# Block sums of the normed input made by 128-feature quarters in five shared buffers, with the homes of three pools turned round

## The chip, the cores and the metric

The kernel runs on one NeuronCore of a Trainium2 chip. Its engines are TensorE (PE in the profile, with its weight loads as PEld), VectorE (DVE), ScalarE (ACT), GpSimd (POOL) and SyncE (SP), which here only issues transfers. Each engine works through its own instructions in the order in which they were written for it, and an instruction that waits for another engine or for a transfer holds everything behind it on its engine. The metric is the device time of one execution in microseconds (us).

## The reference

One layer of a hybrid decoder on 1024 tokens of width 1024 in float32: sandwich norms around two token mixers (a sparse attention and a latent attention) that are merged by sigmoid gates, and around a gated convolutional feed-forward. What matters here is the input projection and the gates:

```python
h = _rmsnorm(x, g_pre_mix[i])
proj = h @ w_in[i]
q_n, kv_n, gate_n, c_q, c_kv, k_r, merge = jnp.split(proj, offsets, axis=-1)
...
gm = jax.nn.sigmoid(merge.astype(jnp.float32)).astype(x.dtype).reshape(B, T, 2, D)
merged = gm[:, :, 0] * (o_nsa @ w_br_nsa[i]) + gm[:, :, 1] * (o_mla @ w_br_mla[i])
```

`merge` has 2048 columns: sixteen output blocks of 128.

## The kernel before

The normed input h is held transposed, features on partitions: `hh` is its high part and `hl` what is left (a float32 value is multiplied as three products of high and low parts, `mm3`, lines 303 to 305). Both stand in two halves of 512 tokens, `hh0`/`hl0` and `hh1`/`hl1`, each of 8 blocks of 128 features.

The stage in question comes after the first token projections. In order of the program:

- the first gate block (`fproj(merge_evac(0))`);
- the latent attention's projections (lines 597 to 652): for each of 8 blocks of 128 tokens `mla_q` and `mla_qt` make queries (tile `qx`), `mla_v` values (`vm`) and `mla_k` keys (`kx`). Each of the three tiles has two buffers, is split into high and low part by ACT and DVE, and is then stored to DRAM by SP (`q_d`, `v_d`, `k_d`);
- three more gate blocks by plain projections, the early projections (`EARLY`, 48 matmuls of 512 columns each);
- ten gate blocks in five pairs by class `Seven`. A pair is a 2 by 2 product of blocks (two gate blocks, two halves of the features, two halves of the tokens) done with seven block products P1 to P7 of 12 matmuls each where eight would be plain (Strassen's scheme in Winograd's form). The products take sums of weight blocks (`S0` to `S3`, line 170, split into `rh`/`rl`, held in a ring of four) and sums of blocks of h: `T1` = B12 - B11, `T2` = B22 - T1, `T3` = B22 - B12, `T4` = B21 - T2, each again as high and low part of 128 x 4 x 512. P5 takes T1, P6 takes T2, P7 takes T3, P4 takes T4; P1, P2 and P3 take plain blocks of h. The T blocks are made once (`t_block`, lines 671 to 678) and serve all five pairs.

A T block is made by DVE and ACT: three DVE operations for the sum (lines 675, 676 and 677: high parts, then each low part), then the split (`split_evac`: ACT copies the high part, line 308, and DVE subtracts it, line 309). Before the change each of these works on 1024 elements per partition, two of the four feature blocks.

The written program is put in order, engine by engine, when it is built: a scheduler places instructions by priority and by what it reckons to be ready. So an edit at one place also changes the order at others.

Memory is handed out by pools that grow from two sides. The pools of the latent attention (`a0`, `a2`) grow from the right and are closed when it is written out. Those of the gates (`tA` for the T blocks, `ringA` for the ring and one weight buffer, `eA` for sums and partial results) grow from the left, into the room that the others leave. A tile that comes to lie where an older tile lay waits until the older one has been read for the last time: by TensorE for weights and inputs, by the store for `qx`, `kx` and `vm`.

Of the kernel before, what the change touches and what calls it, by code (L numbers as in the profile page):

```python
# [8 lines left out]
F32 = mybir.dt.float32  # L9
F32R = mybir.dt.float32r  # L10
# [27 lines left out]
def f32(a):  # L38
    return a.bitcast(F32)
# [236 lines left out]
def tile_hybrid_layer(ctx: ExitStack, tc: tile.TileContext, x, p, positions, g_pre_mix, w_in,  # L276
# [30 lines left out]
    def split_evac(hi, lo, ps):  # L307
        nc.scalar.activation(hi, ps, AF.Copy)  # L308
        nc.vector.tensor_sub(lo, ps, f32(hi))  # L309
# [94 lines left out]
    def two_banks():  # L404
        return ps1([128, 2, 512], F32, "sc", bufs=2)

    hp = Pool("hp", side="right")
    hh, hl = [None, None], [None, None]
# [152 lines left out]
    def fproj(evac):  # L561
        fproj2([evac])

    def merge_evac(m):
        hold = {}

        def run(c, cs, ps):
            if c == 0:
                hold["t"] = gmp([128, T], F32, "gms", bufs=2)
            nc.scalar.activation(hold["t"][:, cs], ps, AF.Sigmoid)  # L570
            if c == 1:
                nc.scalar.dma_start(gm_d[m], hold["t"])
        return run
# [84 lines left out]
    a0.close()  # L658


    tA = Pool("tA", side="left")
    ringA = Pool("ringA", side="left")
    eA = Pool("eA", side="left")
    BA = {n: [tA([128, 4, 512], F32R, n + tag) for tag in "hl"] for n in ("T1", "T2", "T3", "T4")}
    for c in range(2):
        for h in range(2):
            ks = slice(4 * h, 4 * h + 4)
            BA[f"B{h + 1}{c + 1}"] = hh[c][:, ks], hl[c][:, ks]
    gates7 = Seven(nc, W, gate_pairs, ringA, BA, mm3, split_evac)

    def t_block(out_, plus, minus):
        for ks in (slice(0, 2), slice(2, 4)):
            (ah, al), (bh, bl) = ([f32(b[:, ks]) for b in BA[n]] for n in (plus, minus))
            sum_ = eA([128, 2, 512], F32, "sum")
            nc.vector.tensor_tensor(sum_, ah, bh, op=OP.subtract)
            nc.vector.tensor_tensor(sum_, sum_, al, op=OP.add)
            nc.vector.tensor_tensor(sum_, sum_, bl, op=OP.subtract)
            split_evac(BA[out_][0][:, ks], BA[out_][1][:, ks], sum_)

    fproj(merge_evac(EARLY[0]))  # L680
    t_block("T1", "B12", "B11")
    fproj(merge_evac(EARLY[1]))
    t_block("T2", "B22", "T1")
    t_block("T3", "B22", "B12")
    fproj(merge_evac(EARLY[2]))
    for i in range(4):
        gates7.block_sum(0, i)
    for n in range(Seven.RING):
        gates7.prep(n)
    t_block("T4", "B21", "T2")  # L690
    for f in range(len(gate_pairs)):
        tl = [gmp([128, T], F32, "gms", bufs=2) for _ in range(2)]
        gates7.pair(f, two_banks(), bank, eA, [(c[:, :512], c[:, 512:]) for c in tl],
                    lambda out_, ps: nc.scalar.activation(out_, ps, AF.Sigmoid), lambda s: None)
        nc.scalar.activation(tl[1], tl[1], AF.Sigmoid)
        nc.scalar.dma_start(gm_d[PAIRED[2 * f + 1]], tl[1])
        nc.scalar.activation(tl[0][:, 512:], tl[0][:, 512:], AF.Sigmoid)
        nc.scalar.dma_start(gm_d[PAIRED[2 * f]], tl[0])
    for pl in (eA, ringA, tA):
        pl.close()  # L700


# [579 lines left out]
    T1 = []  # L1282
# [32 lines left out]
    for t in (4, 5, 6, 7, 0, 1, 2, 3):  # L1315
        c, lt = t // 4, slice(t % 4 * 128, t % 4 * 128 + 128)
# [212 lines left out]
    left, right = slice(0, 512), slice(512, 1024)  # L1529
# [207 lines left out]
```

## Time and profile before

| | |
|---|---|
| time, median of 3 runs | 1796.21 us (1796.06 to 1799.11) |
| the profiled execution: time, span of its trace | 1803.28 us, 1801.3 us |
| PE busy, share of the span | 1720.6 us, 96% |
| DVE busy | 1274.0 us, 71% |
| ACT busy | 860.7 us, 48% |
| POOL busy | 310.7 us, 17% |

The profiled execution is one run with the profiler on; the median comes from runs of their own. All positions below are microseconds from the start of the trace. TensorE is the engine that is busy nearly throughout, so the question for any stage is where it stands still or runs at the lower of its two clock levels (1.2 and 2.4 GHz).

### The profile page before, as it was taken

What the parts mean: (1) busy time and instruction counts of PE and PEld (TensorE: products, weight loads), DVE (VectorE), ACT (ScalarE), POOL (GpSimd) and SP (SyncE); (2) the same over time, 40 slices, a digit from 0 to 9 for tenths busy, and PEclk for the clock granted to TensorE, in tenths of its full rate; (3) what the DMA queues carried; (4) which work ended last, traced back from release to release, by engine and by line L of the source; (5) the groups of instructions that cost most, each with busy time, mean ns of one, the idle gap of its engine ahead of it and who ended that gap; (6) DMA issues with size and microseconds to landing.
All of it is one profiled execution on the core that took longest, in us unless ns stands there. A gap on an engine that the chain in (4) does not pass through costs nothing.

```text
span 1801.3 us, 23532 instructions
## 1 busy us (share of the span) xinstructions
PE 1720.6 (96%) x8525; PEld 1403.2 (78%) x8525; DVE 1274.0 (71%) x1978; ACT 860.7 (48%) x1532; POOL 310.7 (17%) x467
## 2 busy tenths in 40 slices
PE   8998899999999999999989989999999998999998
PEld 6876678887777787887778867888888876887886
DVE  6456654435888887777764797888888879768453
ACT  6443232235777776666542444444444443345321
POOL 3220003003545544333311000000000000001010
PEclk9999799999999999999999989999999999999999
DMA  5393233200001316757372112222223292438111
GB/s 192 93 281 110 70 110 84 54 28 26 1 1 36 100 59 170 164 136 197 118 245 85 47 59 83 82 82 84 80 82 94 71 345 87 149 118 273 57 59 47
DMA packets 182511, 191.93 MB, mean 107 GB/s; under 512 B 12804, under 2 KB 136124, under 8 KB 182396
## 3 DMA queue, kind: packets, MB, share of 16 engines
q1 hardware_dynamic: 175292, 180.91, 32.9%
q10 hardware_dynamic: 7104, 9.54, 1.6%
q8 instruction: 67, 1.10, 0.3%
q14 instruction: 48, 0.39, 0.1%
HBM read 142.96 MB, written 47.45 MB: 106 GB/s over the span
## 4 chain that ended last, share of the span: by engine, by line
PE 75%; DVE 10%; DMA 8%; ACT 3%; issue 2%; POOL 1%; SPq 1%; DVEq 0%; POOLq 0%; ACTq 0%
PE big L304 9%; PE big L303 9%; PE big L305 9%; PE pT L303 5%; PE pT L304 5%; PE pT L305 5%; PE pT L885 5%; PE one L303 3%; PE one L304 3%; PE one L305 3%; PE oT L895 3%; PE oT L894 3%; PE sc L948 1%; DVE wlo L309 1%; DMA g<-gm_d 1%
## 5 line engine op out<-in xcount | busy, mean ns | idle before, releaser
L345 POOL TENSOR_SCALAR stat<-stat 128x1 f32<-128x1 f32 (+1 forms) x48 | 19.1, 399 | 904.7 <-ACT yn L1278 633.0
L309 DVE TENSOR_TENSOR pl<-pT,ph 128x512 fp32r<-128x512 f32 (+1 forms) x244 | 149.7, 630 | 13.8 <-ACT ph L308 12.0
L308 ACT ACTIVATE ph<-pT 128x512 fp32r<-128x512 f32 (+1 forms) x244 | 130.3, 556 | 60.5 <-PE pT L885 52.7
L303 PE MATMUL big<-hh,rh 128*128 128x512 f32 x364 | 142.3, 391 | 2.2 <-ACT e L220 0.8
L305 PE MATMUL big<-hh,rl 128*128 128x512 f32 x364 | 141.7, 390 | 1.0 <-DVE rl L309 1.0
L304 PE MATMUL big<-hl,rh 128*128 128x512 f32 x364 | 141.9, 390 | 0.0
L869 DVE TENSOR_REDUCE mx<-sc 128x1 f32<-128x640 f32 (+7 forms) x128 | 106.6, 835 | 32.2 <-PE sc L948 22.3
L308 ACT ACTIVATE rh<-S 128x512 fp32r<-128x512 f32 x104 | 65.1, 628 | 120.6 <-PE big L304 80.4
L308 ACT ACTIVATE rh<-wraw 128x512 fp32r<-128x512 f32 x82 | 51.3, 631 | 131.7 <-PE big L304 43.0
L1395 DVE SCALAR_TENSOR_TENSOR u<-C,wcT,u 128x1024 f32<-128x1024 f32 x88 | 110.8, 1279 | 3.6 <-ACT u L1391 3.5
L304 PE MATMUL big<-wlo,whi 128*128 128x512 f32 x242 | 97.3, 402 | 9.4 <-DVE wlo L309 9.3
L305 PE MATMUL big<-whi,wlo 128*128 128x512 f32 x242 | 95.5, 395 | 0.0
L303 PE MATMUL big<-whi 128*128 128x512 f32 x242 | 92.1, 397 | 2.9 <-ACT whi L308 2.9
L303 PE MATMUL pT<-hh,whi 128*128 128x512 f32 x224 | 88.6, 395 | 4.1 <-ACT gms L570 1.6
L305 PE MATMUL pT<-hh,wlo 128*128 128x512 f32 x224 | 87.9, 392 | 0.0
L304 PE MATMUL pT<-hl,whi 128*128 128x512 f32 x224 | 87.8, 392 | 0.0
L309 DVE TENSOR_TENSOR rl<-S,rh 128x512 fp32r<-128x512 f32 x104 | 71.0, 686 | 21.2 <-ACT rh L308 21.2
L303 PEld LDWEIGHTS big<-hh,rh 128*128 128x128 f32 x364 | 68.4, 188 | 17.7 <-ACT e L220 1.2
L305 PEld LDWEIGHTS big<-hh,rl 128*128 128x128 f32 x364 | 68.6, 188 | 15.7 <-DVE rl L309 1.4
L304 PEld LDWEIGHTS big<-hl,rh 128*128 128x128 f32 x364 | 68.5, 188 | 14.5 <-DVE hl L309 0.4
L309 DVE TENSOR_TENSOR rl<-wraw,rh 128x512 fp32r<-128x512 f32 x82 | 56.2, 687 | 21.1 <-ACT rh L308 21.1
L308 ACT ACTIVATE whi<-wraw 128x1024 fp32r<-128x1024 f32 x40 | 42.1, 1058 | 56.9 <-DVE wraw L1464 27.2
(544 smaller groups left out, 5035.4 us busy)
## 6 DMA issues: line engine op xcount, KB each, us to landing
wraw<-in_w_up_dram SPq DMA_DIRECT2D x44, 512.0 KB, 3.9
wraw<-in_w_in_dram SPq DMA_DIRECT2D x24, 512.0 KB, 3.9
g<-gm_d SPq DMA_DIRECT2D x48, 256.0 KB, 3.1
wraw<-in_w_down_dram SPq DMA_DIRECT2D x47, 256.0 KB, 3.3
g_d<-u SPq DMA_DIRECT2D x22, 512.0 KB, 2.6
wraw<-g_d SPq DMA_DIRECT2D x36, 256.0 KB, 3.5
xt<-in_x_dram SPq DMA_DIRECT2D x16, 512.0 KB, 7.5
gm_d<-gms ACTq DMA_DIRECT2D x16, 512.0 KB, 3.4
```

What stands on the lines that cost most here:

```text
L303: nc.tensor.matmul(ps, lh, rh, start=start, stop=False, skip_group_check=more)
L304: nc.tensor.matmul(ps, lh, rl, start=False, stop=False, skip_group_check=more)
L305: nc.tensor.matmul(ps, ll, rh, start=False, stop=stop, skip_group_check=more)
L308: nc.scalar.activation(hi, ps, AF.Copy)
L309: nc.vector.tensor_sub(lo, ps, f32(hi))
L345: nc.gpsimd.tensor_scalar(st, st, EPS, None, op0=OP.add)
L869: nc.vector.tensor_reduce(u.nm[:, r:r + 1], src, axis=AX.XY, op=OP.max, negate=True)
L885: nc.tensor.transpose(pT[:m, r], cols(r), ident)
L894: nc.tensor.matmul(oT[:, a:], v, ph, start=first, stop=False)
L895: nc.tensor.matmul(oT[:, a:], v, pl, start=False, stop=last)
L948: nc.tensor.matmul(ps[:, si, :w], q_part(0, 128, i, 4 * g + r), KA[b - 1][g][:, k0 + o:k0 + o + w], start=False, stop=True)
L1395: nc.vector.scalar_tensor_tensor(u[s], C[s][:, 2 - sh:2 - sh + T], wcT[:, 2 - sh, ch:ch + 1], u[s], op0=OP.mult, op1=OP.add)
```

## The change

The sums are made by quarters: 512 elements per partition instead of 1024, four rounds per T block instead of two. The sum tile, which was one buffer of 128 x 2 x 512, becomes five rotating buffers of 128 x 512 under the name `e`, and the partial results of the pairs (`e1`, `U2`, `U3`), which had buffers of their own, rotate through the same five. `T3` is written after the third early projection and the first weight sums instead of before. The three pools are opened in another order, and the T tiles in the order T2, T3, T4, T1.

```diff
+    eA = Pool("eA", side="left")
+    ringA = Pool("ringA", side="left")
     tA = Pool("tA", side="left")
-    ringA = Pool("ringA", side="left")
-    eA = Pool("eA", side="left")
-    BA = {n: [tA([128, 4, 512], F32R, n + tag) for tag in "hl"] for n in ("T1", "T2", "T3", "T4")}
+    BA = {n: [tA([128, 4, 512], F32R, n + tag) for tag in "hl"] for n in ("T2", "T3", "T4", "T1")}
...
     def t_block(out_, plus, minus):
-        for ks in (slice(0, 2), slice(2, 4)):
-            (ah, al), (bh, bl) = ([f32(b[:, ks]) for b in BA[n]] for n in (plus, minus))
-            sum_ = eA([128, 2, 512], F32, "sum")
+        for k in range(4):
+            (ah, al), (bh, bl) = ([f32(b[:, k]) for b in BA[n]] for n in (plus, minus))
+            sum_ = eA([128, 512], F32, "e", bufs=5)
             nc.vector.tensor_tensor(sum_, ah, bh, op=OP.subtract)
             nc.vector.tensor_tensor(sum_, sum_, al, op=OP.add)
             nc.vector.tensor_tensor(sum_, sum_, bl, op=OP.subtract)
-            split_evac(BA[out_][0][:, ks], BA[out_][1][:, ks], sum_)
+            split_evac(BA[out_][0][:, k], BA[out_][1][:, k], sum_)
...
     t_block("T2", "B22", "T1")
-    t_block("T3", "B22", "B12")
     fproj(merge_evac(EARLY[2]))
     for i in range(4):
         gates7.block_sum(0, i)
     for n in range(Seven.RING):
         gates7.prep(n)
+    t_block("T3", "B22", "B12")
     t_block("T4", "B21", "T2")
     for f in range(len(gate_pairs)):
         tl = [gmp([128, T], F32, "gms", bufs=2) for _ in range(2)]
-        gates7.pair(f, two_banks(), bank, eA, [(c[:, :512], c[:, 512:]) for c in tl],
+        gates7.pair(f, two_banks(), bank, lambda shape, dt, name: eA(shape, dt, "e", bufs=5), [(c[:, :512], c[:, 512:]) for c in tl],
                     lambda out_, ps: nc.scalar.activation(out_, ps, AF.Sigmoid), lambda s: None)
...
-    for pl in (eA, ringA, tA):
+    for pl in (tA, ringA, eA):
         pl.close()
```

The homes, as the built programs place them, in thousands of bytes per partition from the left edge of the room. The older tiles are those of the latent attention. Below 16.9 lie none of them.

| | before | after |
|---|---|---|
| older tiles | | wuh, wul 16.9 to 29.2; wk, wv 29.2 to 37.4; qm, ra, rb 37.4 to 47.6; vm 47.6 to 55.8; kx 55.8 to 64.0; qx 64.0 to 80.4; cth 80.4 to 92.7; ctl 92.7 to 105.0 (same in both) |
| sums and partial results | 94.2 to 104.4 (ctl) | 0 to 10.2 (none) |
| weight buffer of the ring | 65.5 to 69.6 (qx) | 10.2 to 14.3 (none) |
| S0 to S3 | 69.6 to 77.8 (qx) | 14.3 to 22.5 (wuh, wul) |
| rh, rl | 77.8 to 94.2 (qx, cth, ctl) | 22.5 to 38.9 (weights, qm) |
| T1 | 0 to 16.4 (none) | 88.1 to 104.4 (cth, ctl) |
| T2 | 16.4 to 32.8 (wuh, wul, wk) | 38.9 to 55.3 (qm, ra, rb, vm) |
| T3 | 32.8 to 49.2 (wk, wv, qm, ra, rb, vm) | 55.3 to 71.7 (vm, kx, qx) |
| T4 | 49.2 to 65.5 (vm, kx, qx) | 71.7 to 88.1 (qx, cth) |

Three places show how the order moves. The first is on DVE, where the latent attention begins: `krx` is the last split of the token projections, `wul`, `wkl` and `wvl` are splits of the latent attention's weights, `wlo` splits weights of the early projections, `vm_892` is the first tile to be stored. Before:

```order
L309 TENSOR_TENSOR krx_775<-pT_768,krx_775 32x128
L309 TENSOR_TENSOR wul_844<-wraw_247,wuh_843 128x768
L309 TENSOR_TENSOR wul_844<-wraw_251,wuh_843 128x768
L309 TENSOR_TENSOR wkl_846<-wraw_783,wkh_845 128x512
L309 TENSOR_TENSOR wvl_848<-wraw_783,wvh_847 128x512
L107 TENSOR_TENSOR wlo_1315<-wraw_851,whi_1314 128x1024
L309 TENSOR_TENSOR vm_892<-pT_888,vm_892 128x8x64
```

After, from the same split on (behind these rows follow `wvl`, the four L677 of T1, a `wlo`, two `qm` operations and a second `wlo`, and then `vm_892`):

```order
L309 TENSOR_TENSOR krx_775<-pT_768,krx_775 32x128
L675 TENSOR_TENSOR e_1380<-hh1_122,hh0_124 128x512
L675 TENSOR_TENSOR e_1386<-hh1_122,hh0_124 128x512
L675 TENSOR_TENSOR e_1392<-hh1_122,hh0_124 128x512
L675 TENSOR_TENSOR e_1398<-hh1_122,hh0_124 128x512
L676 TENSOR_TENSOR e_1380<-e_1380,hl1_123 128x512
L309 TENSOR_TENSOR wul_844<-wraw_247,wuh_843 128x768
L676 TENSOR_TENSOR e_1386<-e_1386,hl1_123 128x512
L309 TENSOR_TENSOR wul_844<-wraw_251,wuh_843 128x768
L676 TENSOR_TENSOR e_1392<-e_1392,hl1_123 128x512
L309 TENSOR_TENSOR wkl_846<-wraw_783,wkh_845 128x512
L676 TENSOR_TENSOR e_1398<-e_1398,hl1_123 128x512
```

All twelve sums of T1 moved from behind the latent attention to its beginning, between the weight splits.

The second is on PE in the first pair, behind P1 and P3 (the last P3 matmul is the first row). Before, P6 (bank `pT_1653`) begins with one matmul on T2, and P2 on plain blocks (`sc_1572` from `hh0`) stands in front of the rest:

```order
L305 MATMUL pT_1612<-hh1_122,rl_1551 128x512
L303 MATMUL pT_1653<-T2h_1308,rh_1585 128x512
L303 MATMUL sc_1572<-hh0_124,rh_1544 128x512
L304 MATMUL sc_1572<-hl0_125,rh_1544 128x512
L305 MATMUL sc_1572<-hh0_124,rl_1545 128x512
L303 MATMUL sc_1572<-hh0_124,rh_1544 128x512
```

After, P6 (`pT_1701`) and P7 (`pT_1722`, which takes T3) stand there entire, and P2 (`sc_1620` from `hh0`, `rh_1556`) follows behind both:

```order
L305 MATMUL pT_1660<-hh1_122,rl_1563 128x512
L303 MATMUL pT_1701<-T2h_1306,rh_1633 128x512
L304 MATMUL pT_1701<-T2l_1307,rh_1633 128x512
L303 MATMUL pT_1722<-T3h_1308,rh_1653 128x512
L304 MATMUL pT_1722<-T3l_1309,rh_1653 128x512
L305 MATMUL pT_1701<-T2h_1306,rl_1634 128x512
```

So P7 moved ahead of P2, of the second pair's P1 and of P5.

The third is on DVE where T2 ends. Before, T2's halves follow each other operation by operation, and T3 comes behind all of T2:

```order
L309 TENSOR_TENSOR T1l_1307<-sum_1386,T1h_1306 128x1024
L675 TENSOR_TENSOR sum_1454<-hh1_122,T1h_1306 128x1024
L676 TENSOR_TENSOR sum_1454<-sum_1454,hl1_123 128x1024
L677 TENSOR_TENSOR sum_1454<-sum_1454,T1l_1307 128x1024
L309 TENSOR_TENSOR T2l_1309<-sum_1454,T2h_1308 128x1024
```

After, the last split of T2 (`T2l` from `e_1484`, first row) is followed by the quarters of T3 and T4 in a mix; the last split of T3 (`T3l` from `e_1588`) is the 26th instruction, counting this row as the first:

```order
L309 TENSOR_TENSOR T2l_1307<-e_1484,T2h_1306 128x512
L675 TENSOR_TENSOR e_1582<-hh1_122 128x512
L309 TENSOR_TENSOR T3l_1309<-e_1570,T3h_1308 128x512
L676 TENSOR_TENSOR e_1576<-e_1576,hl1_123 128x512
L309 TENSOR_TENSOR rl_1634<-S1_1546,rh_1633 128x512
L675 TENSOR_TENSOR e_1588<-hh1_122 128x512
L675 TENSOR_TENSOR e_1594<-hh0_124,T2h_1306 128x512
L676 TENSOR_TENSOR e_1582<-e_1582,hl1_123 128x512
```

T4's sums (`e_1594`, `e_1600`) and the second pair's weight sums now stand between T3's quarters.

## Rows read from the trace of the kernel before

**Rows 1.** Windows: busy time of each engine, granted clock, DMA share, GB/s
```profile
88.00:140.00 52.00, 48.08 (x248) 40.31 (x247) 26.30 (x38) 23.23 (x37) 10.32 (x24) 1.00 1.00 285
119.40:211.90 92.50, 77.19 (x288) 58.60 (x289) 64.69 (x74) 28.47 (x41) 0.00 (x0) 0.87 0.42 121
...
200.00:210.00 10.00, 6.88 (x14) 4.29 (x15) 5.72 (x7) 2.74 (x3) 0.00 (x0) 0.50 0.13 49
```

**Rows 2.** Timeline of PE: start, duration, instruction, idle before it and its releaser
```profile
117.97 1.04 PE L627 MATMUL sc<-ident,qm 128*96 128x128 f32 x8
119.46 0.50 PE L303 MATMUL pT<-hh,whi 128*128 128x512 f32 x1 [0.46 <-DVE kx L309]
...
130.87 0.39 PE L303 MATMUL pT<-hh,whi 128*128 128x512 f32 x1
...
141.75 0.39 PE L303 MATMUL pT<-hh,whi 128*128 128x512 f32 x1
...
149.00 0.50 PE L303 MATMUL pT<-hh,whi 128*128 128x512 f32 x1 [1.65 <-ACT gms L570]
...
164.56 0.80 PE L303 MATMUL pT<-T2h,rh 128*128 128x512 f32 x1 [4.38 <-ACT rh L308]
...
202.36 0.79 PE L303 MATMUL pT<-T4h,rh 128*128 128x512 f32 x1 [2.84 <-ACT T4h L308]
```

**Rows 3.** Timeline of ACT and of DVE: the longest waits of the stretch
```profile
147.31 1.15 ACT L308 ACTIVATE rh<-wraw 128x512 fp32r<-128x512 f32 x2 [13.44 <-DMA q_d<-qx]
...
147.32 0.69 DVE L170 TENSOR_TENSOR S<-wraw 128x512 f32<-128x512 f32 x1 [9.12 <-DMA q_d<-qx]
```

**Rows 4.** Timeline of DVE: T2's first half, and T4's last split
```profile
159.16 1.23 DVE L675 TENSOR_TENSOR sum<-hh,T1h 128x1024 f32<-128x1024 f32 x1
160.42 1.22 DVE L676 TENSOR_TENSOR sum<-sum,hl 128x1024 f32<-128x1024 f32 x1
...
202.34 1.22 DVE L309 TENSOR_TENSOR T4l<-sum,T4h 128x1024 fp32r<-128x1024 f32 x1 [1.12 <-ACT T4h L308]
```

**Rows 5.** Timeline of DVE at the start of the latent attention
```profile
76.72 0.68 DVE L309 TENSOR_TENSOR wvl<-wraw,wvh 128x512 fp32r<-128x512 f32 x1
81.56 1.23 DVE L107 TENSOR_TENSOR wlo<-wraw,whi 128x1024 fp32r<-128x1024 f32 x1 [4.15 <-ACT whi L106]
```

**Rows 6.** Timeline of DVE: operations of 512 columns, one after another
```profile
178.67 0.68 DVE L194 TENSOR_TENSOR gms<-sc,U 128x512 f32<-128x512 f32 x1
179.27 0.68 DVE L309 TENSOR_TENSOR rl<-S,rh 128x512 fp32r<-128x512 f32 x1
...
207.37 0.68 DVE L194 TENSOR_TENSOR U<-pT,e 128x512 f32<-128x512 f32 x1
208.08 0.69 DVE L194 TENSOR_TENSOR U<-pT,U 128x512 f32<-128x512 f32 x1
```

**Rows 7.** Timeline of ACT: an early projection's sigmoid
```profile
131.81 0.58 ACT L570 ACTIVATE gms<-pT 128x512 f32<-128x512 f32 x1
```

**Rows 8.** Timeline of PE behind the stop at 164.56 us
```profile
166.49 0.63 PE L303 MATMUL sc<-hh,rh 128*128 128x512 f32 x1
166.92 0.63 PE L304 MATMUL sc<-hl,rh 128*128 128x512 f32 x1
...
167.97 0.40 PE L304 MATMUL sc<-hl,rh 128*128 128x512 f32 x1
```

**Rows 9.** Tile qx: its splits (ns min/median/max, starts), its stores' time to landing
```profile
L308 ACT ACTIVATE qx<-sc x8: 1022/1024/1026, 87.6 to 128.9; 96x1024 fp32r<-96x1024 f32 x8
L309 DVE TENSOR_TENSOR qx<-sc,qx x8: 1220/1221/1222, 88.7 to 129.9; 96x1024 fp32r<-96x1024 f32 x8
...
DMA to landing us min/median/max: 6.6/7.2/9.6
```

**Rows 10.** Timeline of PE, all idle times from 330 to 450 us
```profile
354.18 0.33 PE L764 MATMUL pT<-w2t,gl 64*63 64x64 f32 x2 [0.69 <-DVE V L309]
356.01 0.79 PE L303 MATMUL pT<-hh,whi 128*128 128x512 f32 x1 [1.50 <-DVE Vc L309]
```

## The prediction

> **What bounds the kernel now.** TensorE is busy for 96% of the span, so I looked for the stage in which it is not, by the windows. In the stretch from 119.4 to 211.9 us [rows 1] TensorE has 288 matmuls of 512 columns: the three early projections (144) and the first two pairs' products (144). At full rate such a matmul takes 0.227 us: 48 of them lie between 130.87 and 141.75 [rows 2]. 288 would take 65.3 us and the stretch is 92.5 long, so 27.2 us are lost. The granted clock in it is 0.87 on the mean, and 0.50, the lower level (1.2 GHz), from 200 to 210 [rows 1].
>
> The timelines say why, in two steps. First, the latent attention's stores: from 88 to 140 the DMA engines are full, at 285 GB/s [rows 1]. ACT and DVE stand until 147.3 for a store of `qx` [rows 3], for 13.4 and 9.1 us, because the ring's homes lie where `qx` lay. TensorE works through the early projections meanwhile and stops 1.65 us only when ACT doesn't empty its bank [rows 2]. Second, what DVE could not do in that time it does afterwards: T1 to T4, one after another, the last split ending at 203.6 [rows 4]. TensorE, whose products take them, stops 4.38 us in front of T2, 2.84 in front of T4's last half [rows 2], with others between, and runs at the lower level behind the stops: at 166.49 two matmuls start 0.43 apart, until 167.97 [rows 8]. So the stage is bound by DVE's T blocks, and by stores that make DVE begin late.
>
> **The change, part by part.** I follow one point, the end of those 288 matmuls, and keep the clock of the trace before; a lag of the whole stage is added at the end.
>
> *Homes.* The sums and the weight buffer now lie where nothing lay, the ring where weights lay that TensorE has read by 117.97 [rows 2], T1 over its inputs `cth` and `ctl`, also read then. The wait of rows 3 is gone for all of them. T3 and T4 now lie on `kx` and `qx` and wait for the last stores, which landed by 147.3; they need their homes only at 154 (below). That slack of 7 us hides this wait; were it gone, each microsecond would pass to TensorE.
>
> *T1's sums.* Twelve operations move to the start of the latent attention. DVE operations of 512 columns that don't wait start 0.60 apart, dependent ones 0.71 [rows 6], so they take 7.2 us. DVE idled 4.15 us there, between the last weight split and 81.56 [rows 5]; so the first splits for the stores come some 3 us late. The stores then fill the DMA engines as before, so a late start is a late end; but other loads feed the engines meanwhile. I take a lag of 2.0, bounds 0 (all hidden) and 7.2 (nothing hidden).
>
> *Quarters.* 64 DVE operations of 512 columns take the place of 32 of 1024. A half with dependent operations starts the next after 1.26 [rows 4], two quarters after 1.20: no cost, some gain. The chain of one block also breaks up, since the order puts other quarters between. Here the Trainium skill speaks against the change: "VectorE: DVE Perf Modes", in its section on the TRN2 errata, says that every VectorE instruction pays a fixed latency, so that many small tiles pay it many times, and gives (N + 151)/0.96 ns for a float32 operation on two tensors, 0.69 for 512 and 1.22 for 1024. The single durations agree (0.68 and 1.22), the distances between starts don't; by the formula the 32 more operations would cost an estimated 5.0 us of DVE, by the rows nothing.
>
> *T2.* ACT works in order, and T1's and T2's copies now stand between the sigmoids of the early projections. The last quarter of T2 comes behind the last sigmoid. Early projections: 119.46 plus 144 matmuls (32.6), plus the eight transposes that now stand inside the first of them (1.04 [rows 2]): 153.1. The sigmoid of 0.58 [rows 7], then T2's last copy of about the same length: 154.4. T1 and most of T2 are done by then in DVE's free time.
>
> *T3, which is late next.* From T2's last split to T3's last split DVE has 26 instructions of 512 columns; at 0.60 they end at 154.4 + 15.6 = 170.0. TensorE has P1 and P3 (24 matmuls, 5.4) done at 158.5, and then P6 and P7, with P2 behind them. Of these it can do 22 matmuls (5.0) before T3's last quarter: it stops for 170.0 - 158.5 - 5.0 = 6.5 us, in pieces.
>
> *Shared buffers.* ACT's copy of P1 takes the buffer that T3's last quarter frees, so ACT stands there until 170.0, and the second pair's weight split behind it. P2 waits for that copy, but it stands behind P7, which ends then anyway: 0, and 0.6 if P7 came earlier.
>
> *T4.* Its last split is 13 instructions behind T3's, 177.8. TensorE has 38 matmuls (8.6) in front of it: 178.6. Covered, by little.
>
> *Clock.* The stop of 4.38 us cost seven matmuls at 0.43 instead of 0.23, 1.4 us [rows 8]. The stops up to 202.36 cost a window of 10 us at the lower level [rows 1], at most 5.0. T3's stop is in pieces, between the two: 3.0.
>
> I add 0.5 for splits of the second pair that DVE does late. The sum of what is lost after: lag 2.0, transposes 1.0, T3's stop 6.5, clock 3.0, rest 0.5: 13.0. Of 27.2 lost before, 14.2 come back. Behind the stretch TensorE is the bound: from 330 to 450 it idles 0.69 and 1.50 us, both times for DVE work that moves along [rows 10]. So the gain stays. The profiled execution took 1803.28 (span 1801.3), 7.1 above the median; it would take 1789.1, and the median run 1796.2 - 14.2 = **1782.0 us**.
>
> **The rivals.**
>
> *T3 is in time.* DVE is busy 64.7 of 92.5 us in the stretch [rows 1] and loses 7.2 of that, so its work is not too much in sum. If it runs ahead and T3 stops nothing, 6.5 and the clock's 3.0 come back too: 1772.5. Against it stands the count of 26. Chance 0.13.
>
> *Quarters cost their full length.* If each operation starts when the one before has ended, 26 take 17.9 instead of 15.6 and T1's sums 8.3 instead of 7.2: 3.4 more, 1785.4. The durations speak for it (0.68), the starts of rows 6 against it. It is what the skill's formula for VectorE amounts to. Chance 0.12.
>
> *The stores lag by all of T1's sums.* 7.2 instead of 2.0: 1787.2. For it: the DMA engines stay full from 88 to 140. Chance 0.12.
>
> *The gain is given back.* If a later stage waits for something that doesn't move along, 1796. Rows 10 show no such wait. Chance 0.07.
>
> *Slower: the stores stop overlapping.* With the order moved, the splits of `qx` come two at a time. A store lands 7.2 us after its issue; with the two splits in front (1.0 and 1.2 [rows 9]) a block of 128 tokens would take 9.4 us if it waited for its own store, against 6.4 now (1.8 MB by the tiles' shapes, at 285 GB/s). For six of the eight blocks that is 18 us, more than the 14.2: 1800. It decides from 2.4 us a block. Against it: each of the three tiles still has its two buffers, and the DMA engines were full all the while [rows 1], which no change of order among the same stores takes away by itself. Chance 0.08.
>
> **How the numbers follow.** The case above has 0.48, with a range of its own from 1778 to 1787 (clock 1.4 to 5.0, lag 0 to 5). The first rival sets the low end, 1772; the second and third lie inside or near 1787. With the upper end at 1793 the last two, 0.15, are left out. A measurement of this kernel tells about 0.2%, 3.6 us, from no change. Faster by more than that: 0.48 + 0.13 + 0.12 + 0.12 = 0.85, of which I give 0.01 to no change; same 0.08; slower 0.08.
>
> **What would show it.** No wait of ACT or DVE for `qx` stores by the ring; first early projection some 2 us later than 119.46; PE stops in front of P7, released by T3's splits, of 6 to 7 us in sum, and none of size in front of T4; DVE instructions there 0.60 apart; the 288 matmuls ending near 198. Wrong it would be if the latent attention got longer by more than 7 us, if P7 did not wait, or if a stop appeared behind the pairs that was not there before.

## The result, and the profile after

The changed kernel took 1785.26 us (median of 4 runs, 1783.92 to 1788.58), the kernel before in the same comparison 1797.66 (4 runs, 1796.06 to 1801.34): a ratio of 0.9931, 95% interval 0.9909 to 0.9953, 12.4 us faster where 14.2 were predicted. A second comparison (6 runs against 23) gave 0.9919, 0.9895 to 0.9942. The profiled execution after took 1785.98 us (span 1784.0), against 1803.28 (1801.3) before: PE is busy for 1714.9 us of it, DVE 1275.4, ACT 862.6.

Windows of after: bounds and length of the window, busy time (and instructions) of PE, PEld, DVE, ACT and POOL, granted clock, DMA share and GB/s. The second runs from the first early projection to the end of the 288 matmuls, as the second of [rows 1] does.

```profile
88.00:140.00 52.00, 45.47 (x229) 38.95 (x230) 25.71 (x42) 24.37 (x40) 13.63 (x30) 0.93 0.94 265
126.86:202.88 76.02, 71.03 (x297) 57.05 (x297) 59.49 (x95) 29.53 (x49) 0.04 (x1) 0.93 0.53 150
170.00:180.00 10.00, 5.14 (x11) 3.33 (x12) 10.00 (x18) 4.82 (x9) 0.00 (x0) 0.64 0.21 52
180.00:190.00 10.00, 10.00 (x39) 8.05 (x39) 7.62 (x13) 3.57 (x7) 0.00 (x0) 0.85 0.00 0
```

The stretch is 76.0 us long instead of 92.5 [rows 1]; it starts 7.4 us later. Within it the clock is low only between 170 and 190: 0.64 in the first ten microseconds, where DVE is busy throughout, and 0.85 in the next ten.

Timeline of PE, after. In the whole stretch PE stops three times, all in front of `T3`:

```profile
126.86 0.50 PE L303 MATMUL pT<-hh,whi 128*128 128x512 f32 x1
131.76 1.03 PE L627 MATMUL sc<-ident,qm 128*96 128x128 f32 x8
...
170.70 0.51 PE L303 MATMUL pT<-T3h,rh 128*128 128x512 f32 x1 [0.79 <-ACT T3h L308]
174.01 0.80 PE L304 MATMUL pT<-T3l,rh 128*128 128x512 f32 x1 [2.80 <-DVE T3l L309]
...
177.02 0.79 PE L304 MATMUL pT<-T3l,rh 128*128 128x512 f32 x1 [1.36 <-DVE T3l L309]
...
182.73 0.57 PE L305 MATMUL sc<-hh,rl 128*128 128x512 f32 x1
183.13 0.40 PE L303 MATMUL sc<-hh,rh 128*128 128x512 f32 x1
```

The stops in front of T2 and T4 and the one for ACT's `gms` [rows 2] are gone. Behind the stop at 177.02 matmuls start 0.43 apart until 183.13, as in [rows 8].

Timeline of DVE, after: the start of the latent attention, to compare with [rows 5], and T2's last and T3's last split.

```profile
75.64 2.48 DVE L675 TENSOR_TENSOR e<-hh,hh 128x512 f32<-128x512 f32 x4
...
82.80 0.67 DVE L309 TENSOR_TENSOR wvl<-wraw,wvh 128x512 fp32r<-128x512 f32 x1
83.40 2.48 DVE L677 TENSOR_TENSOR e<-e,hl 128x512 f32<-128x512 f32 x4
...
88.62 0.53 DVE L619 TENSOR_TENSOR qm<-ra,rb 128x128 f32<-128x128 f32 x1 [1.61 <-POOL rb L618]
89.08 0.54 DVE L620 TENSOR_TENSOR qm<-ra,rb 128x128 f32<-128x128 f32 x1
89.54 1.48 DVE L107 TENSOR_TENSOR wlo<-wraw,whi 128x1024 fp32r<-128x1024 f32 x1
90.94 0.68 DVE L309 TENSOR_TENSOR vm<-pT,vm 128x512 fp32r<-128x512 f32 x1
...
158.43 0.69 DVE L170 TENSOR_TENSOR S<-wraw 128x512 f32<-128x512 f32 x1 [1.68 <-DMA wraw<-in_w_in_dram]
...
162.42 0.69 DVE L309 TENSOR_TENSOR T2l<-e,T2h 128x512 fp32r<-128x512 f32 x1 [0.29 <-ACT T2h L308]
...
177.48 0.69 DVE L309 TENSOR_TENSOR T3l<-e,T3h 128x512 fp32r<-128x512 f32 x1
```

From T2's last split to T3's last are 25 steps in 15.06 us, 0.60 each. `wvl`, at 76.72 before, comes at 82.80, and the first stored tile (`vm`) 8.2 us later than at 82.70.

Timeline of ACT, after: the last copy of `qx` still waits for an older store; T1's copies stand behind the sigmoids of the first early projection, and the ring's `rh` goes on without the wait of [rows 3].

```profile
135.13 1.02 ACT L308 ACTIVATE qx<-sc 96x1024 fp32r<-96x1024 f32 x1 [2.15 <-DMA q_d<-qx]
...
140.72 2.20 ACT L308 ACTIVATE T1h<-e 128x512 fp32r<-128x512 f32 x4 [0.40 <-ACT gms L570]
142.82 1.14 ACT L308 ACTIVATE rh<-wraw 128x512 fp32r<-128x512 f32 x2
```

Timeline of PE, after: the waits that answer to [rows 10] are the same two, 12.1 us earlier.

```profile
342.06 0.33 PE L764 MATMUL pT<-w2t,gl 64*63 64x64 f32 x2 [0.69 <-DVE V L309]
...
343.89 0.80 PE L303 MATMUL pT<-hh,whi 128*128 128x512 f32 x1 [1.50 <-DVE Vc L309]
```

Timeline of PE, before: two stops in the later pairs, behind the stretch, which after doesn't have.

```profile
229.01 0.50 PE L303 MATMUL sc<-hh,rh 128*128 128x512 f32 x1 [0.49 <-ACT rh L308]
249.99 0.50 PE L303 MATMUL sc<-hh,rh 128*128 128x512 f32 x1 [1.64 <-DVE S L170]
```

So the account of the two profiled executions up to there is: the stretch starts 7.4 us later, is 16.5 shorter, and behind it 3.0 more are gained, 2.1 of them by these two stops; what makes up the rest was not traced. That is 12.1. From there to the end the spans differ by 5.2 us more, in lines that the change doesn't touch; over the twelve traces of this study that tail, which begins at 298.60 in after, takes from 1484.4 to 1490.6 us, and kernels that don't differ from the change there have both ends of it (1490.3 with the sums midway, 1484.4 with the copies first).

### The profile page after: what moved, and what is told of

The parts are those of the page before. It is cut to its first block, busy times and chain, and to the rows that moved or that the text cites. A ratio compares the mean times of both kernels' runs of the same rounds, so it can differ in the third digit from the quotient of the medians.

```text
span 1784.0 us, 23567 instructions
## 1 busy us (share of the span) xinstructions
PE 1714.9 (96%) x8525; PEld 1403.9 (79%) x8525; DVE 1275.4 (71%) x2010; ACT 862.6 (48%) x1540; POOL 312.5 (18%) x467
## 4 chain that ended last, share of the span: by engine, by line
PE 77%; DVE 9%; DMA 6%; ACT 3%; issue 2%; POOL 1%; SPq 1%; DVEq 0%; ACTq 0%; POOLq 0%
PE big L304 9%; PE big L305 9%; PE big L303 9%; PE pT L303 6%; PE pT L305 6%; PE pT L304 6%; PE pT L885 5%; PE one L303 3%; PE one L304 3%; PE one L305 3%; PE oT L895 3%; PE oT L894 3%; PE sc L948 1%; DVE wlo L309 1%; PE sc L941 1%
## 5 line engine op out<-in xcount | busy, mean ns | idle before, releaser
L869 DVE TENSOR_REDUCE mx<-sc 128x1 f32<-128x640 f32 (+7 forms) x128 | 106.6, 835 | 32.3 <-PE sc L948 22.5
L308 ACT ACTIVATE rh<-S 128x512 fp32r<-128x512 f32 x104 | 65.1, 629 | 116.3 <-PE big L304 80.6
L304 PEld LDWEIGHTS big<-hl,rh 128*128 128x128 f32 x364 | 68.5, 188 | 14.6 <-DVE hl L309 0.4
```

The costliest lines, as they stand in the source:

```text
L304: nc.tensor.matmul(ps, lh, rl, start=False, stop=False, skip_group_check=more)
L869: nc.vector.tensor_reduce(u.nm[:, r:r + 1], src, axis=AX.XY, op=OP.max, negate=True)
```

## The experiments

One part needed no run: built with `T3` written at its old place, the changed program has the same order on PE, DVE and ACT. Of the five edits four are left: homes, order of the T tiles, quarters, five buffers.

Every trace is read at the same points, us from its start: DVE's first split of `vm`, its last split of `qx`, the first early projection, the start of the 288th matmul behind that, and the distance from the second to the fourth.

| kernel | first vm | last qx | first early | 288th | qx to 288th | GB/s, 88 to 140 | ratio to before |
|---|---|---|---|---|---|---|---|
| before | 82.70 | 129.94 | 119.46 | 211.51 | 81.6 | 285 | |
| before, second trace | 83.88 | 138.73 | 127.84 | 219.33 | 80.6 | 246 | |
| before, third trace | 83.79 | 132.79 | 123.33 | 210.34 | 77.6 | 275 | |
| after | 90.94 | 136.19 | 126.86 | 202.65 | 66.5 | 265 | 0.9931 |
| after, second trace | 90.19 | 136.41 | 127.03 | 202.78 | 66.4 | 266 | 0.9919 (0.9895 to 0.9942) |
| homes alone | 82.33 | 129.43 | 120.36 | 207.17 | 77.7 | 276 | 0.9960 (0.9939 to 0.9980) |
| quarters alone | 83.19 | 137.06 | 125.42 | 212.68 | 75.6 | 247 | 0.9949 (0.9931 to 0.9968) |
| pools exchanged | 84.33 | 134.71 | 123.95 | 205.70 | 71.0 | 270 | 0.9933 (0.9911 to 0.9956) |
| sums midway | 84.62 | 134.03 | 129.97 | 202.99 | 69.0 | 276 | 0.9935 (0.9908 to 0.9961) |
| copies first | 91.08 | 136.30 | 126.23 | 196.36 | 60.1 | 265 | 0.9881 (0.9852 to 0.9910) |
| sums in advance | 84.02 | 140.15 | 129.22 | 195.25 | 55.1 | 253 | 0.9865 (0.9835 to 0.9895) |
| sums all at the start | 97.22 | 142.88 | 133.48 | 199.61 | 56.7 | 241 | 0.9882 (0.9835 to 0.9929) |

**The changed kernel again**, unedited.

> The changed kernel once more, to see which of its differences come back. In its first trace the clock was 0.89 from 60 to 76 us, ahead of the change, and the last transposes of the token projections came 1.8 us later than before; between 917 and 1760 us a further 5.2 us were gained in lines that the change doesn't touch. If both belong to single executions, this trace shows the early projections at about 125 instead of 126.9, and a gap to before that stays at 12 to 14 us from 290 us to the end. If they belong to the kernel, both come back.

Both came back: the early projections started at 127.03, the whole stretch repeated within 0.2 us, and the gap to the first trace of before is 12.0 at 298.71 and 17.6 at the end. Of the offset ahead of the change 1.1 us came back (`krx` at 74.70, against 73.64 in the first trace of before and 75.44 in the first of after); the two later traces of before have it at 74.81 and 74.73, so it isn't the change's. That neither tail nor late start is the kernel's alone came out only with further traces, of before and of edited kernels, below.

**Homes alone**, against the kernel before:

```diff
-    tA = Pool("tA", side="left")
+    eA = Pool("eA", side="left")
     ringA = Pool("ringA", side="left")
-    eA = Pool("eA", side="left")
+    tA = Pool("tA", side="left")
...
-    ... for n in ("T1", "T2", "T3", "T4")}
+    ... for n in ("T2", "T3", "T4", "T1")}
```

> The kernel before with the homes of the three pools and the T tiles turned as in the change; sums still by halves in one buffer. Theory one (the gain comes from the homes: no wait for the stores of qx): DVE goes on with T1 at about 135 instead of 147.3, T4's last split comes some 12 us earlier, at about 192 to 195, and of the 12.4 us gained by the whole change 8 to 12 are there. Only three sums of a half, 3.7 us of DVE, stand ahead of the latent attention, so by the view that the sums delay it the first early projection comes at about 122 (3 us late, half as late as in the change). Rival (the gain comes from the quarters and five buffers, which break the chain sum, copy, split): 0 to 3 us gained.

0.9960: some 7 us by the ratio, 4 to 11 by its interval, so the 8 to 12 are not excluded by the time alone. But T4's last split missed its forecast: the wait of [rows 3] is gone, and another takes its place. Timeline of DVE, homes alone:

```profile
152.66 0.69 DVE L170 TENSOR_TENSOR S<-wraw 128x512 f32<-128x512 f32 x1 [9.78 <-DMA wraw<-in_w_in_dram]
153.27 1.22 DVE L677 TENSOR_TENSOR sum<-sum,hl 128x1024 f32<-128x1024 f32 x1
155.61 1.22 DVE L309 TENSOR_TENSOR T1l<-sum,T1h 128x1024 fp32r<-128x1024 f32 x1 [1.13 <-ACT T1h L308]
```

The first weight sum of the second pair stands in DVE's order in front of the last sum of T1's second half. Its weights are loaded by SP behind the stores, so DVE stands 9.78 us with T1 unfinished, and T4's last split comes at 199.84, only 2.5 us earlier than in [rows 4], where 7 to 10 were forecast. Pools and T tiles were turned together here, so their shares are not told apart.

**Quarters alone**, against the kernel before:

```diff
-        for ks in (slice(0, 2), slice(2, 4)):
-            (ah, al), (bh, bl) = ([f32(b[:, ks]) for b in BA[n]] for n in (plus, minus))
-            sum_ = eA([128, 2, 512], F32, "sum")
+        for k in range(4):
+            (ah, al), (bh, bl) = ([f32(b[:, k]) for b in BA[n]] for n in (plus, minus))
+            sum_ = eA([128, 512], F32, "e", bufs=5)
...
-        gates7.pair(f, two_banks(), bank, eA, ...
+        gates7.pair(f, two_banks(), bank, lambda shape, dt, name: eA(shape, dt, "e", bufs=5), ...
```

> The kernel before with the sums by quarters in five rotating buffers; homes as before. Theory one: the wait for the stores of qx until 147 stays, T2 to T4 start behind it; at 0.60 per operation T3's last split comes at about 182 and T4's at 190, PE stops some 20 us in pieces for T3, and 0 to 5 us are gained. Early projections start at 119.5, without lag. Rival (the quarters carry the gain): 9 us gained or more, since T4 is done 13 us earlier than before with the stores' wait still there.

0.9949: some 9 us, 6 to 12 by the interval: more than theory one said, and at the lower end of what the rival said. The store wait stays, as ACT's timeline of quarters alone shows:

```profile
154.20 1.16 ACT L308 ACTIVATE rh<-wraw 128x512 fp32r<-128x512 f32 x2 [8.47 <-DMA q_d<-qx]
```

Timeline of DVE, quarters alone, T1's first split and T4's last two:

```profile
154.82 0.69 DVE L309 TENSOR_TENSOR T1l<-e,T1h 128x512 fp32r<-128x512 f32 x1
...
195.50 1.29 DVE L309 TENSOR_TENSOR T4l<-e,T4h 128x512 fp32r<-128x512 f32 x2 [0.27 <-ACT T4h L308]
```

From T1's first to T4's last split it takes 41.3 us (154.82 to 196.11), against 53.8 before (148.53 to 202.34). The two stops behind the stretch (229.01 and 249.99 in before) stand in every trace with halves, homes alone too, and in none with quarters. So homes and quarters each bring a part of like size (7 and 9 us), and together 12.4 and 14.6 by the two comparisons, about what both bring alone within the intervals. Neither carries the whole gain by itself.

**The pools of the sums and of the ring exchanged**, against the changed kernel:

```diff
-    eA = Pool("eA", side="left")
     ringA = Pool("ringA", side="left")
+    eA = Pool("eA", side="left")
     tA = Pool("tA", side="left")
```

> The changed kernel with the sums' pool and the ring's pool exchanged: the sums now lie where weights and qm lay, so T1's twelve sums stand behind the latent attention again; the ring lies at the bottom; the T tiles stay. My theory after the result: the twelve sums ahead of the latent attention's own DVE work delay it by some 5.6 us, more than the 2.0 predicted, and here the first early projection is back at 119.5. DVE has room for the sums during the early projections, so T3 comes no later against the projections than in the change: 6 us more gained than with the change at least, and up to 12 if T3's stop goes as well. Rival (the lag is the price for having T1 early, and T3's stop grows by as much): the same time as the change, within 2 us.

0.9933, the same as the change within the interval; the 6 us didn't come. The sums moved further than I had reckoned. Timeline of DVE, pools exchanged:

```profile
134.71 1.22 DVE L309 TENSOR_TENSOR qx<-sc,qx 96x1024 fp32r<-96x1024 f32 x1 [3.37 <-ACT qx L308]
...
137.20 2.49 DVE L675 TENSOR_TENSOR e<-hh,hh 128x512 f32<-128x512 f32 x4
```

They stand behind the last split of `qx`, which waits for stores, and T1's splits begin at 148.03 instead of 142.21. The first early projection came at 123.95, not at 119.5, and T1's splits 5.8 us later, so nothing was left of it at the end. That a lag by itself could be won back was not tested here, since its premise, projections at 119.5, did not come about.

**The kernel before, a second and a third trace**, unedited.

> The kernel before, profiled once more. In the four traces so far whose latent attention has the order of before or the order of the change, the first early projection starts anywhere from 119.5 to 127.0, and in the trace of quarters the stores move 226 GB/s from 100 to 140 against 275 in the first trace of before, with the same order of stores. If the stream of stores differs from execution to execution, this trace shows a start of the early projections away from 119.5, up to 125; then part of the 7.4 us by which the change is later there is not the change's. If it is 119.5 again within 1 us, the lag is all the change's.

> The kernel before, profiled a third time, to see how far its stream of stores differs: in its first trace DVE's last split of qx came at 129.9 and the first early projection at 119.5, in its second at 138.7 and 127.8. If the first was the odd one, this trace shows 134 to 139 and 124 to 128; if the second was, 129 to 131 and 119 to 121. The distance from the last split of qx to the 288th matmul should be the same as in both others, 80.6 to 81.6.

The same program with the same order of stores starts its early projections at 119.46, 127.84 and 123.33. Windows of the second trace:

```profile
88.00:140.00 52.00, 42.87 (x220) 35.70 (x218) 25.66 (x40) 21.72 (x35) 10.56 (x25) 0.97 0.89 246
```

Timeline of DVE in the second trace, the last split of `qx`:

```profile
138.73 1.22 DVE L309 TENSOR_TENSOR qx<-sc,qx 96x1024 fp32r<-96x1024 f32 x1 [3.06 <-ACT qx L308]
```

Timeline of PE in the second trace, the first early projection:

```profile
127.84 0.50 PE L303 MATMUL pT<-hh,whi 128*128 128x512 f32 x1 [1.08 <-DVE kx L309]
```

The transfers moved 246 GB/s instead of 285, and everything behind them came some 8 us later than in the first trace. The DMA share fell with the rate, from 1.00 [rows 1] to 0.89: most of the difference is time in which DMA engines were not busy (276 against 285 GB/s per busy share), not slower transfers. The trace on which the prediction rests was the fastest of the three there. The distance from the last split of `qx` to the 288th matmul was not quite the same (the third is 3 us shorter than the second, with a stop of 1.17 where the others have 4.38), but 11 us and more longer than after.

**T1's sums midway**, against the changed kernel (`marks[3]` is DVE's fourth split of `vm`; the line only sets the order of issue):

```diff
+        marks[t] = nc.cur_bb.bb.instructions[-1]
...
+    with tc.issue_after(marks[3]):
         t_block("T1", "B12", "B11")
```

> The changed kernel with T1's sums held on DVE until the fourth split of vm has been issued: homes, buffers and all else stay. They no longer stand between the weight splits at the start of the latent attention. Theory one (the lag is a term that adds up): first early projection 4 to 6 us earlier than in the change, at 121 to 123, and the whole kernel 4 to 6 us faster than the change. Theory two (what sets the end of the stage is DVE's chain of T blocks, which starts behind the last split of qx, and so behind the stores, at about 137 to 141 whatever PE does): the early projections start as early, but PE's stop for T3 grows by the same 4 to 6 us; 288 matmuls end at 202 to 204 as in the change; the same time within 2 us.

The first split of `vm` is back at 84.62, the 288th matmul comes at 202.99 as in the change (202.65), and the ratio is the change's, as the second theory said. It did not come about in its way: the early projections came no earlier, which neither theory had said, and PE's stops shrank to 3.28 us instead of growing. So the first theory's premise was not met either. Timeline of PE, midway:

```profile
128.37 1.94 PE L627 MATMUL sc<-ident,qm 128*96 128x128 f32 x8 [4.66 <-DVE qm L620]
...
174.23 0.50 PE L304 MATMUL pT<-T3l,rh 128*128 128x512 f32 x1 [1.07 <-DVE T3l L309]
...
177.25 0.79 PE L304 MATMUL pT<-T3l,rh 128*128 128x512 f32 x1 [2.05 <-DVE T3l L309]
```

The last transposes of `qm` wait 4.66 us for a DVE operation, which in DVE's order stands behind a split of `qx` that waits for a store. In the change these transposes are issued inside the first early projection, at 131.76, and stop nothing.

**T1's copies first**, against the changed kernel (the sigmoids of the first early projection are issued on ACT behind the last of T1's copies):

```diff
-    fproj(merge_evac(EARLY[0]))
     t_block("T1", "B12", "B11")
+    fproj(merge_evac(EARLY[0], nc.cur_bb.bb.instructions[-2]))
...
+            with tc.issue_after(after) if after else ExitStack():
+                nc.scalar.activation(hold["t"][:, cs], ps, AF.Sigmoid)
```

> The changed kernel with ACT's four copies of T1 ahead of the two sigmoids of the first early projection, behind which they stood at 140.7 to 142.9. Theory two (DVE's chain from T1's splits on sets the end): T1's copies come at 136 to 137, right behind the last copy of qx, T3's last split 3 to 4 us earlier than 177.5, PE's stop of 5 us for it shrinks to 1 to 2, and the matmuls at half rate behind it become fewer: 3 to 6 us faster than the change. Theory one (lag, T3's stop and clock are terms of their own): 0 to 2 us, as the sigmoids that now come later hold a bank.

0.9881; the 288th matmul comes at 196.36, 6.3 us earlier than in the change, a little over the 3 to 6 that the second theory said. Timeline of ACT, copies first:

```profile
139.17 2.18 ACT L308 ACTIVATE T1h<-e 128x512 fp32r<-128x512 f32 x4
141.25 1.08 ACT L571 ACTIVATE gms<-pT 128x512 f32<-128x512 f32 x2
```

Timeline of PE, copies first, around T3:

```profile
170.69 0.50 PE L305 MATMUL pT<-T3h,rl 128*128 128x512 f32 x1 [0.55 <-DVE rl L309]
...
172.50 0.50 PE L304 MATMUL pT<-T3l,rh 128*128 128x512 f32 x1 [0.38 <-DVE T3l L309]
...
173.70 0.50 PE L304 MATMUL pT<-T3l,rh 128*128 128x512 f32 x1 [0.23 <-DVE T3l L309]
```

T1's copies came only 1.55 us earlier (a weight split of ACT still stands in front), but the order of DVE's operations behind them changed too: from T1's first to T3's last split they take 31.3 us (141.65 to 172.94) instead of 35.3, with 53 operations and no wait where the change has 56 and 1.98 us of waits. PE's stops in the stretch shrank from 4.95 to 1.94 us (0.78 of them in front of the second early projection), and no matmul behind them runs at the lower clock.

**T1's and T3's sums in advance**, against the changed kernel: the sums of both go to a pool `xA` of two 8 KB tiles at the bottom, issued behind the second and the fifth split of `vm`; T3's low part and T4's high part rotate into those tiles; T4's low part, T2, T1 and T3's high part get the room from `kx` up.

```diff
+    with tc.issue_after(marks[1]):
+        t_sums("T1", "B12", "B11")
+    with tc.issue_after(marks[4]):
+        t_sums("T3", "B22", "B12")
     fproj(merge_evac(EARLY[0]))
-    t_block("T1", "B12", "B11")
+    t_split("T1")
...
     t_block("T2", "B22", "T1")
+    BA["T3"][1] = xA([128, 4, 512], F32R, "x", bufs=2)
+    t_split("T3")
...
+    BA["T4"][0] = xA([128, 4, 512], F32R, "x", bufs=2)
     t_block("T4", "B21", "T2")
```

> A version meant to be faster than both. T1's and T3's sums (24 DVE operations, T3 needs neither T1 nor T2) are made in two tiles of their own during the latent attention, T1's behind the second split of vm, T3's behind the fifth, where DVE waits for ACT and ACT for the stores; those tiles then take T3's low part and T4's high part; T2, T1 and T4's low part get the homes that fit. Theory two: behind the latent attention DVE has 12 operations fewer ahead of T3, and T3's split comes before T2's, at about 150 to 155; PE stops neither for T3 nor runs at half rate; the 288 matmuls end at 189 to 193 instead of 202.7, and the kernel is 9 to 13 us faster than the change. Theory one: 5 us from the lag, 5 from the stop and 4 from the clock: 14. If the sums delay the splits that are stored, the early projections start as late as in the change, and about 5 us of it are lost.

0.9865, faster than before by 24 us (1777.91 and 1802.31) and than the change by 10 to 12 by the ratios. Windows of sums in advance, from the first early projection to the end of the 288 matmuls:

```profile
129.22:195.48 66.26, 66.26 (x298) 54.87 (x297) 51.10 (x82) 28.31 (x48) 0.00 (x0) 1.00 0.55 156
```

Not one stop, full clock, 66.3 us for 288 matmuls and eight transposes. So here the stretch ends 66 us after it starts, and its start alone sets its end. The 288 matmuls end at 195.5, not at 189 to 193: of theory one's parts, the stop and the clock came, the lag didn't, as the early projections start at 129.22. Whether that is this execution's stream (253 GB/s) or the 24 sums inside the latent attention is not shown. Whether these runs are faster than those with the copies first is not settled: the intervals overlap.

**All 24 sums at the start**: sums in advance, without the two lines that hold them back.

```diff
-    with tc.issue_after(marks[1]):
-        t_sums("T1", "B12", "B11")
-    with tc.issue_after(marks[4]):
-        t_sums("T3", "B22", "B12")
+    t_sums("T1", "B12", "B11")
+    t_sums("T3", "B22", "B12")
```

> The version in advance with T1's and T3's 24 sums left to the scheduler, which puts nearly all of them ahead of the latent attention's first split of vm: twice as many as in the change, 14.4 us of DVE where the change has 7.2. If the latent attention's start adds to its end one to one (the lag as a term, 7 us for 12 sums), the first split of vm comes at 96 to 98 and the last split of qx at 142 to 146, 6 us and more later than in the change, and the kernel is 4 to 7 us slower than the version in advance. If the stores take the delay up, because they move faster when less waits for them at once, the last split of qx comes at 136 to 141 and the time is that of the version in advance within 3 us.

Timeline of DVE, all sums at the start:

```profile
97.22 0.68 DVE L309 TENSOR_TENSOR vm<-pT,vm 128x512 fp32r<-128x512 f32 x1
...
142.88 1.22 DVE L309 TENSOR_TENSOR qx<-sc,qx 96x1024 fp32r<-96x1024 f32 x1 [2.85 <-ACT qx L308]
```

The first split of `vm` comes 13.2 us later than with the sums in advance, the last split of `qx` 2.7, the 288th matmul 4.4, and the medians lie 5.4 apart (1783.26 and 1777.91, in two comparisons; 3 us by the ratios, whose intervals overlap). The marks set for "one to one" were met: 97.22, 142.88 and 5.4 us. But the sums in advance are a late reference themselves (last `qx` at 140.15), so this pair shows a fifth to a third of the 13.2 us passed on; against the mean of the three traces of before, 9.1 of 13.8 are. With single traces and 8.8 us between the traces of before, that share stays open. The table shows one thing more. From the first split of `vm` to the last of `qx` it takes 45.2 to 46.2 us in the four traces with the sums at the start (after twice, copies first, all at the start), and 47.1 to 56.1 in the eight others: part of the late start is made up on the way.

## Why the prediction was right, and where not

The path that it named is the path that was measured: the store wait goes, DVE's chain of T blocks starts earlier, and T3's last split is what TensorE waits for next. With the lag of 7.4 us in the first pair of traces put in, its times for T2's and T3's last splits (154.4 and 170.0) come to 161.8 and 177.4; measured, the two splits start at 162.42 and 177.48. The number is in part luck, since misses in both directions cancelled, as follows.

- **The store wait in front of the ring** is gone, as forecast; the stores of `qx` nowhere hold the ring or a T block. But the step that took it for the whole gate failed: with the homes alone DVE stands 9.78 us at the next load in the queue. I had followed the stores and not what SP issues behind them, the weights of the second pair. In the change that wait is 1.68 us (158.43), since with quarters DVE has more of T1 and T2 to do first: it is busy 10.32 of the 12 us from 147 to 159, against 2.22 of the 12 from 141 to 153 with the homes alone.
- **Quarters cost nothing**: right, 0.60 a step over 25 steps. By the formula in the Trainium skill, "VectorE: DVE Perf Modes", its section on the TRN2 errata, an operation takes 0.69 us, as the trace's duration says; but the next one starts 0.09 earlier than that, so its extra cost, an estimated 5.0 us, did not come about. What I had put down as "some gain" brings some 9 us when made alone.
- **T1's sums, the lag.** The first stores come 6.4 us late, not 3: from `krx` to the first `vm` it is 9.06 in each of the three traces of before and 15.5 in both of after. The 4.15 us of idle time [rows 5] covered less than I thought: the idle time was behind the weight splits and the sums were put between them, DVE still waits 1.61 us at 88.62 for `rb`, and two operations for `qm` and a second `wlo`, 2.3 us, now stand ahead of the first `vm`. The lag at the end of the latent attention looks like 7.4 us in the first pair of traces. Against the mean of the three traces of before it is 2.5 at the last split of `qx` and 3.4 at the first early projection, with 8.8 between the traces of before themselves. Counted from `krx`, the latent attention itself is 5.6 longer in the first pair and 2.7 on the mean (45.8, 53.0 and 48.6 before, 51.4 and 52.3 after), so the sign of being wrong that was set at 7 did not appear. So 2.0 is in keeping with that, and its size is not settled better. Nor is the rival that the stores lag by all of T1's sums: the shorter latent attention of the four traces with the sums at the start speaks against it, the spread of the traces doesn't exclude it.
- **T3 is next to be late**: right in place and releaser, 4.95 us instead of 6.5, in three pieces. T4 stops nothing.
- **Clock**: right in place, somewhat larger: 17 matmuls from 174.01 to 183.13, without the stop between them 7.76 us instead of 3.86: 3.9, where 3.0 was taken and 1.4 to 5.0 allowed.
- **Transposes inside the early projections**: 0.79 (131.76 to 132.55) for 1.04. The rest: 76.0 less 65.3, 0.79, 4.95 and 3.9 leaves 1.1, for 0.5.
- **The stretch** without the lag was to be 76.3 us long (92.5 less 16.2) and was 76.0, in part by luck: T3's stop was 1.5 shorter than forecast, clock and rest 1.5 longer together. That it ended at 202.88 and not near 198 is the late start.
- **Behind the stretch** a term was missing: 3.0 us, with the stops at 229.01 and 249.99. I had looked for waits from 330 us on only. Quarters and shared buffers came together in all runs, so which of them removes these stops stays open.

What the whole comes to: the forecast of 14.2 stands against 12.4 and, by the second comparison's ratio, 14.6. At the point where the tail begins, the three traces of before (309.24 to 318.96) and the two of after (298.60 and 298.71) lie 14.3 apart on the mean.

The theory that I formed on the first pair of traces, a lag of 5.6 us to be won back, did not come true in the runs that took the sums from the start (pools exchanged, midway): the time stayed. It is not refuted by them, since neither brought the early projections back to 119.5. What sets the end of the stage in the change is the chain behind the last split of `qx`: T1's copies, then DVE's operations up to T3's last split, 37 us without a pause over 2 us (140.72 to 177.48). The runs that shorten it, copies first and the two with T3's sums made ahead, are those that gain on the change (the last of them with an interval that overlaps the change's). Once the chain is short enough, the start counts in full: in the two with T3's sums made ahead the 288th matmul comes 66.0 and 66.1 us after the first early projection. Why the same transfers move at 246 GB/s in one execution and 285 in another, with the DMA engines busy 0.89 and 1.00 of the window, stays open.

## What to carry to other kernels

When a wait for a store is taken away, look up what is next in the same queue: here it was a weight load behind the stores, and only other work placed in front of it made the freed time usable. Look where in the idle stretch moved work will stand: between operations that others wait for, it delays them although the engine idles right behind. A lag read from one trace on each side is no result where a stage runs at the pace of its transfers: trace the kernel before two or three times, and measure from the end of the stream.

## What the runs showed of the hardware

The same program's stream of stores, same order and same sizes, differed from execution to execution by 16% (246, 275 and 285 GB/s from 88 to 140 us, at DMA shares of 0.89, 0.97 and 1.00), and the stage behind it moved by up to 9 us with it. The spans of these three executions followed: 1806.7, 1799.6 and 1801.3 us. How much of the spread of the kernel before comes from this, whose runs lay between 1794.28 and 1811.24 us, is not shown.

VectorE operations of 512 columns in the chain start 0.60 us apart (25 steps in 15.06 us), while each is recorded with 0.69 us.

Stops of 2.80 and 1.36 us went with 17 matmuls mostly 0.43 us apart instead of 0.227 (granted clock 0.64 from 170 to 180); with stops of 0.55, 0.38 and 0.23 us in the same place (copies first) none ran at the lower level.
